# Two interleaved opening products, sums of squares by tokens, and small fp32 matmuls ahead of the first product and around the last sums

## The chip, the cores and the metric

The kernel runs on one core of one Trainium2 chip. The core has engines that run side by side, each with its own instruction queue, in order: TensorE (PE in the profile, with its weight loads as PEld), VectorE (DVE), ScalarE (ACT), GpSimd (POOL) and SyncE (SP), which here only starts transfers (DMAs). The metric is the device time in microseconds (us) of one execution, as a median of runs; lower is better.

## The reference

One inference step of an encoder trunk with two layers for 512 prompt tokens and 8 x 16 sample tokens, 640 tokens of width 1024 in all. Each layer is

```
x += 1/2 * SwiGLU_1(RMSNorm(x))
x += mixer(RMSNorm(x))          # short convolution, band attention, gates
x += 1/2 * SwiGLU_2(RMSNorm(x))
```

and a last RMSNorm follows. `RMSNorm(x) = x * rsqrt(mean(x*x) + 1e-6) * g`, and `SwiGLU(h) = (silu(h @ w_g) * (h @ w_u)) @ w_down` with an inner width of 2816. The mean is over the 1024 features of a token.

## The kernel before

x lies in SBUF by features: eight rows `x[0]` to `x[7]`, each 128 features (partitions) by T = 640 tokens. Products need fp32 accuracy and are made from a faster format (fp32r): an operand is split into a high part (a cast, on ScalarE) and a low part (the rest, a subtraction on VectorE), and one product of a 128 x 128 weight tile is three matmuls (high x high, low x high, high x low) for each half of the tokens (HT = 320). Since the norm's factor belongs to a token, i.e. a column, the products run on `x * g` and their results are scaled by the factor (rho) later.

Weights come as a stream of slabs of 128 x 1024 (512 KB), `wst`. `load` starts the transfer of a slab into one of a few buffers `raw` on SP's queue; `prep` casts it (`whi`) and notes the subtraction (`wlo`), which `flush` issues on VectorE; `slab` and `Tiles.take` hand the prepared slab out and prepare two ahead; `quiet` hands out without preparing. `wlo` and `whi` have three buffers each.

The first FFN of the first layer (`ffn("a0")`) starts with `opening` (L602): four inner tiles j, a gate and an up product each, so 2n = 8 products of 8 x 6 = 48 matmuls (L372). Each takes all eight rows of x. Their PSUM results are `acc` tiles of two banks, of which there are two (`layout("f", 1)`), so product i needs the buffer of product i - 2, which `out(i - 2)` has to have read: for the first pair a copy on ScalarE, for later ones a scaling by rho on VectorE (`scaled`, L487). The other four banks are `att` tiles. The rows of the opening run in the order in which they are written, on TensorE, VectorE and ScalarE (`order(ORDERED)`).

Before: x and the first slab come in alternating transfers (L415, L421). For each row, ScalarE and VectorE make its parts `hhi`, `hlo`, and for every second row two tiles of the first slab. Product 0 takes rows as they come; then product 1 with slab 1. Squares of the eight rows are made on ScalarE (L574) and added on VectorE (L578). Within product 2 the sums over features are made by ten small matmul instructions (`npsa`, L472), root and reciprocal follow, and the factors are put on a diagonal (L482); after the first row of product 3 a fp32 product with ones (`nbca`, L595) spreads them over the partitions, and ScalarE copies them to `rho` (L597). Meanwhile `final(m)` builds the operands `xhi`, `xlo` of the later inner tiles (seven combinations of row pairs: even row m in slots 5 and 6, odd row in 3 and 4, combinations of both in 0 to 2), spread over the products by the table `made`.

At the very end, `Final.all` (L1877) makes the last down product in two parts of the tokens (A, 384, and B, 256); it squares on ScalarE, sums over features by small matmuls with ones (`add`, L1936), takes root, reciprocal and diagonal (`root`, `turn`), spreads them (`spread`, L1952) and writes `yout` (`out`, L1957). The last rows of B end the kernel.

Of the kernel before, what the change touches and what calls it, by code (L numbers as in the profile page):

```python
# [10 lines left out]
F32 = mybir.dt.float32  # L11
# [5 lines left out]
P = 128  # L17
# [160 lines left out]


@with_exitstack  # L180
def trunk(ctx: ExitStack, tc: tile.TileContext, xin, wst, small, pbias, samplebias, kcache, vcache,
          yout, ko, vo, co):
    nc = tc.nc
    PE, DVE, ACT, POOL, SP = nc.tensor, nc.vector, nc.scalar, nc.gpsimd, nc.sync
# [123 lines left out]
    def flush():  # L308
        for lo, src, hi in pending:
            DVE.tensor_tensor(out=lo, in0=src, in1=hi.bitcast(F32), op=ALU.subtract)  # L310
        pending.clear()
# [94 lines left out]
    POOL.memset(epst, EPS)  # L406
    early = cp.tile([P, 1], F32, name="early")

    less = cp.tile([P, L * KT], F32, name="less")
    POOL.tensor_scalar(out=less, in0=sm[:, O_GM : O_GM + L * KT], scalar1=-1.0, scalar2=None, op0=ALU.mult)  # L410

# [2 lines left out]
    for k in range(KT):  # L414
        SP.dma_start(x[k], xin[:, k, :])  # L415

        if k == 0:
            raws.append(wp.tile([P, CH], F32, tag="raw", name="raw0", bufs=3))
        if k % 2 == 0:
            c = slice(k * P, (k + 2) * P)  # L420
            SP.dma_start(raws[0][:, c], wst[0][:, c])  # L421

    def norm(pool, name, goff, ssum):

# [64 lines left out]
    class Expand(Stats):  # L489
# [10 lines left out]
            self.sq = self.rest = None  # L500
            self.known = False

        def final(self, m, square=True):

            kp, odd = divmod(m, 2)
            n = f"{self.name}_{kp}"
            if not odd:

                self.E = self.fp.tile([P, 3, HT], F32, name=f"xe{n}", tag="even", bufs=1)
                hi = self.fp.tile([P, 7, HT], F32R, name=f"xhi{n}", tag=f"xhi{kp}")  # L510
                lo = self.fp.tile([P, 7, HT], F32R, name=f"xlo{n}", tag=f"xlo{kp}")
                self.ops.append((hi, lo))
# [8 lines left out]
            ACT.activation(B, halves(x[m]), AF.Copy, scale=g)  # L521
            if square and end:
                self.sq = tmp(f"sq{self.name}_{m}")
            elif square:
                self.square(m)
            if not odd:
                DVE.tensor_tensor(out=E[:, 1], in0=E[:, 0], in1=E[:, 2], op=ALU.subtract)
                self.flush()
                ACT.copy(hi[:, 5:7], E[:, 0:2])
                self.late.append((lo[:, 5:7], E[:, 0:2], hi[:, 5:7]))  # L530
            else:
                self.flush()
                ACT.copy(hi[:, 3:5], O[:, 3:5])
                for o, a, b in ((XN6, E[:, 1], O[:, 4]), (XT4, O[:, XN6], O[:, 3])):
                    DVE.scalar_tensor_tensor(out=O[:, o], in0=a, scalar=-1.0, in1=b,
                                             op0=ALU.mult, op1=ALU.subtract)
                DVE.tensor_tensor(out=O[:, XT7], in0=O[:, 4], in1=E[:, 2], op=ALU.subtract)
                self.late.append((lo[:, 3:5], O[:, 3:5], hi[:, 3:5]))
                self.flush()

                def rest():
                    ACT.copy(hi[:, 0:3], O[:, 0:3])
# [5 lines left out]
                if not end:  # L548
# [53 lines left out]
    def opening(fp, name, goff, n, put, tails):  # L602

        ACT.copy(early, epst)
        ex = Expand(fp, name, goff)
        h = []
        whi, wlo = (wp.tile([P, CH], F32R, tag=f"w{t}", name=f"w{t}0", bufs=3) for t in ("hi", "lo"))
        ready.append((whi, wlo))  # L610
        for k in range(KT):
            g = sm[:, goff + k : goff + k + 1]
            hi = hp.tile([P, T], F32R, tag="hhi", name=f"hhi{name}_{k}")
            lo = hp.tile([P, T], F32R, tag="hlo", name=f"hlo{name}_{k}")
            ACT.activation(hi, x[k], AF.Copy, scale=g)
            c = slice(k * P, (k + 2) * P)
            if k % 2 == 0:
                ACT.copy(whi[:, c], raws[0][:, c])
            DVE.scalar_tensor_tensor(out=lo, in0=x[k], scalar=g, in1=hi.bitcast(F32),
                                     op0=ALU.mult, op1=ALU.subtract)  # L620
            if k % 2 == 0:
                DVE.tensor_tensor(out=wlo[:, c], in0=raws[0][:, c], in1=whi[:, c].bitcast(F32),
                                  op=ALU.subtract)
            h.append((hi, lo))
        flush()

        made = {2: (0, 1), 3: (2, 3), 4: (4,), 5: (5, 6), 6: (7,)}
        us, gs, ps = [], [], []

        def out(i):  # L630

            j, up = divmod(i, 2)
            if not up:
                gs.append(tmp(f"g{name}_{j}"))
                if j:
                    scaled(gs[j], ps[i], ex.rho)
                    ACT.activation(gs[j], gs[j], AF.Silu)
# [11 lines left out]
        def begun():  # L649
            ex.total(att(f"nps{name}"))  # L650
            ex.root()
            ex.diagonal()

        at = {2: {4: begun}, 3: {1: lambda: ex.spread([att(f"nbc{name}_{a}")[:, :HT] for a in range(2)])}}
        for i in range(2 * n):
            ps.append(acc(f"po{name}_{i}"))
            product(ps[i], h, at.get(i, {}))
            if i > 1:
                out(i - 1)
            if i == 0:  # L660
                for k in range(KT):
                    ex.square(k)
                    ex.add()
                    if k == 1:
                        out(0)
                    if k == 4:
                        flush()
            if i == 1:
                continue
            if i == 3:  # L670
                g, u = gs[0], us[0]
                DVE.tensor_tensor(out=g, in0=g, in1=ex.rho, op=ALU.mult)
                ACT.activation(g, g, AF.Silu)
                DVE.tensor_tensor(out=u, in0=u, in1=ex.rho, op=ALU.mult)
            flush()
            for m in made.get(i, ()):
                ex.final(m, False)
            if i == 3:
                DVE.tensor_tensor(out=u, in0=u, in1=g, op=ALU.mult)
            if i == max(made):  # L680
                ex.rest()
        ahead()
        begin()
        out(2 * n - 1)

        def parts(j, u):
# [1181 lines left out]
    class Final:  # L1868
# [8 lines left out]
        def all(self, ops):  # L1877
# [9 lines left out]
            for m in range(KT):  # L1887
# [9 lines left out]
                    ACT.copy(rr, self.spread(0))  # L1897
                if m == 5:
                    self.ps = acc("npsf1")[:, :, 0]
                    self.add(self.ssum[1], True)  # L1900
                if m > 4:
                    self.add(self.sq)
# [158 lines left out]
def _layout(inputs):  # L2061
# [21 lines left out]
    return {"xin": xin, "wst": _stream(i), "small": small, "pbias": pbias, "samplebias": sbias, "kcache": kc, "vcache": vc}  # L2083


_OUTS = {
# [39 lines left out]
```

## Time and profile before

| | |
|---|---|
| median of three runs | 2496.47 us (2495.63 to 2496.84) |
| the profiled execution | 2496.66 us |
| its span, first to last instruction | 2494.7 us |
| mean granted TensorE clock | 0.998 |

The page of the profile gives the busy time of each engine, the chain of waits that ended last, and groups of instructions. Closer views are the timeline of one engine (start, duration, engine, line, operation, output <- inputs, shape, count, and in brackets the idle time before and what ended it), the chain within a stretch, and windows (busy time of each engine in order PE, PEld, DVE, ACT, POOL, then the granted clock, the share of the DMA engines and GB/s). Line numbers are those of the kernel before. Starts on one engine can lie closer together than the durations say, since instructions overlap in its pipeline.

### The profile page before, as it was taken

The numbers are of one execution on the slowest core, as the hardware profiler recorded it, in microseconds if no ns is written. First come the engines' busy times: TensorE is split into PE (matmuls) and PEld (weight loads), VectorE is DVE, ScalarE is ACT, GpSimd is POOL, SyncE is SP. The second block draws the span as 40 slices with busy tenths as digits, with TensorE's granted clock in tenths as the row PEclk, the third lists the DMA queues.
The fourth block names the chain that finished last, engine by engine and source line by source line (L and its number), as shares of the span: only waits on it lengthen the run. The fifth ranks groups of instructions, "written<-read, shape, count | busy, mean of one in ns | idle before, by whom it ended". The sixth has DMA issues, their size and how long they took to land.

```text
span 2494.7 us, 43515 instructions
## 1 busy us (share of the span) xinstructions
PE 2478.1 (99%) x17048; PEld 2419.0 (97%) x17048; DVE 2119.2 (85%) x3322; ACT 1450.0 (58%) x2343; POOL 370.7 (15%) x445
## 2 busy tenths in 40 slices
PE   9999999999999999999999999999999999999998
PEld 8999999888999999999999999998899999999998
DVE  7888888878888899888798889888788888989887
ACT  7455556674666555555565555556646665555554
POOL 0011211211111011111001111221111110111111
PEclk9999999999999999999999999999999999999999
DMA  4245665335345344655435555643344553455554
GB/s 146 82 107 124 138 135 130 106 115 167 99 119 145 101 116 118 138 135 135 117 90 126 129 134 123 138 119 115 125 153 104 126 141 95 119 133 122 129 135 110
DMA packets 133261, 308.10 MB, mean 124 GB/s; under 512 B 12768, under 2 KB 76128, under 8 KB 133056
## 3 DMA queue, kind: packets, MB, share of 16 engines
q1 hardware_dynamic: 68976, 219.18, 27.3%
q0 software_dynamic: 63360, 85.50, 20.6%
q8 instruction: 133, 2.18, 0.4%
q10 hardware_dynamic: 720, 0.65, 0.1%
q14 instruction: 72, 0.59, 0.1%
HBM read 221.13 MB, written 7.94 MB: 92 GB/s over the span
## 4 chain that ended last, share of the span: by engine, by line
PE 94%; DVE 3%; ACT 2%; DMA 1%; issue 0%; SPq 0%; DVEq 0%; ACTq 0%
PE pab L395 12%; PE paa L395 11%; PE pcb L395 6%; PE pca L395 6%; PE daa L962 5%; PE dab L962 5%; PE po L372 4%; PE qa L395 4%; PE pbb L395 3%; PE pba L395 3%; PE dca L962 3%; PE dcb L962 3%; PE pda L372 2%; PE pv L1622 2%; PE ma_cv L395 2%; PE qc L395 2%
## 5 line engine op out<-in xcount | busy, mean ns | idle before, releaser
L310 DVE TENSOR_TENSOR wlo<-raw,whi 128x512 fp32r<-128x512 f32 (+1 forms) x583 | 598.6, 1030 | 236.1 <-ACT whi L305 230.6
L305 ACT CAST whi<-raw 128x512 fp32r<-128x512 f32 (+1 forms) x583 | 519.9, 897 | 348.0 <-PE pbb L395 44.6
L305 ACT CAST whi<-s 128x1024 fp32r<-128x1024 f32 (+1 forms) x164 | 153.6, 937 | 248.1 <-issue 107.8
L395 PE MATMUL pab<-xhib,whi 128*128 128x320 f32 x704 | 218.3, 310 | 0.4 <-DVE gb L249 0.4
L395 PE MATMUL pab<-xhib,wlo 128*128 128x320 f32 x704 | 217.4, 309 | 0.0
L395 PE MATMUL pab<-xlob,whi 128*128 128x320 f32 x704 | 217.4, 309 | 0.0
L395 PE MATMUL paa<-xhia,whi 128*128 128x320 f32 x640 | 198.0, 309 | 0.2 <-DVE ga L249 0.2
L395 PE MATMUL paa<-xloa,whi 128*128 128x320 f32 x640 | 197.6, 309 | 0.0
L395 PE MATMUL paa<-xhia,wlo 128*128 128x320 f32 x640 | 197.6, 309 | 0.0
L310 DVE TENSOR_TENSOR wlo<-s,whi 128x1024 fp32r<-128x1024 f32 (+1 forms) x164 | 176.6, 1077 | 10.4 <-ACT whi L305 10.4
L395 PEld LDWEIGHTS pab<-xhib,whi 128*128 128x128 f32 x704 | 132.2, 188 | 1.1 <-DVE gb L249 0.9
L395 PEld LDWEIGHTS pab<-xlob,whi 128*128 128x128 f32 x704 | 132.2, 188 | 0.2
L395 PEld LDWEIGHTS pab<-xhib,wlo 128*128 128x128 f32 x704 | 132.2, 188 | 0.0
L395 PEld LDWEIGHTS paa<-xhia,whi 128*128 128x128 f32 x640 | 120.2, 188 | 0.5 <-DVE ga L249 0.5
L395 PEld LDWEIGHTS paa<-xloa,whi 128*128 128x128 f32 x640 | 120.2, 188 | 0.1
L395 PEld LDWEIGHTS paa<-xhia,wlo 128*128 128x128 f32 x640 | 120.2, 188 | 0.0
L249 DVE TENSOR_TENSOR raw<-raw,raw 128x512 f32<-128x512 f32 x164 | 112.2, 684 | 1.8 <-DMA raw<-in_wst 0.2
L249 DVE TENSOR_TENSOR raw<-s,raw 128x512 f32<-128x512 f32 x164 | 112.3, 685 | 0.0
L395 PE MATMUL pcb<-xhib,whi 128*128 128x320 f32 x352 | 108.7, 309 | 0.0
L395 PE MATMUL pcb<-xlob,whi 128*128 128x320 f32 x352 | 108.7, 309 | 0.0
L395 PE MATMUL pcb<-xhib,wlo 128*128 128x320 f32 x352 | 108.7, 309 | 0.0
L986 POOL DMA_DIRECT2D x<-c_b x52 | 62.6, 1203 | 309.5 <-ACT c_b L979 134.5
(816 smaller groups left out, 8170.8 us busy)
## 6 DMA issues: line engine op xcount, KB each, us to landing
raw<-in_wst SPq DMA_DIRECT2D x375, 512.0 KB, 3.7
x<-c_b POOLq DMA_DIRECT2D x52, 320.0 KB, 5.1
x<-c_a POOLq DMA_DIRECT2D x50, 320.0 KB, 5.0
kc<-in_kcache SPq DMA_DIRECT2D x32, 256.0 KB, 4.1
vc<-in_vcache SPq DMA_DIRECT2D x16, 512.0 KB, 4.5
ub<-cbb POOLq DMA_DIRECT2D x42, 160.0 KB, 5.9
ua<-cba POOLq DMA_DIRECT2D x38, 160.0 KB, 5.4
x<-u_a POOLq DMA_DIRECT2D x18, 320.0 KB, 5.1
```

What stands on the lines that cost most here:

```text
L249: DVE.tensor_tensor(out=out, in0=a, in1=b, op=ALU.add)
L305: ACT.copy(hi[:, d], src[:, c])
L310: DVE.tensor_tensor(out=lo, in0=src, in1=hi.bitcast(F32), op=ALU.subtract)
L372: PE.matmul(ps[a] if isinstance(ps, list) else ps[:, a, :HT], w, x[:, a * HT : (a + 1) * HT], start=first and j == 0, stop=last and j == 2)
L395: PE.matmul(ps, a, b, start=start and kp == 0 and j == 0, stop=stop and kp == NP - 1 and j == 2, skip_group_check=True)
L962: PE.matmul(ps[u], w, y, start=start and i == 0 and j == 0, stop=i == 1 and j == 2, skip_group_check=True)
L986: POOL.dma_start(rows(r, cols), z, accum_op=ALU.add)
L1622: PE.matmul(pv[t], xx[:, t * P : (t + 1) * P], w[:, kk * AW : (kk + 1) * AW], start=c == 0 and kk == 0 and j == 0, stop=c == KT // 2 - 1 a ...
```

## The change

A new input `xtok` holds x by tokens: five tiles of 128 tokens x 1024 features. In the opening:

- `stir` issues 24 fp32 matmuls of ones by ones (128 x 128 by 128 columns) on TensorE, into an `att` tile that nothing reads, ahead of the first product.
- Two slabs are loaded and split along with the rows of x, and products 0 and 1 are interleaved row by row (the last two rows together).
- The odd rows' parts are written to their place in `xhi`, `xlo` at once (`place`), and `final` with `whole=False` no longer makes them.
- The squares are summed over the features of a token by `square(c)`: instructions with an accumulated output, three token tiles on VectorE and two on ScalarE. `npsa` and the squares by rows are gone.
- `spread` and the scaling of the first pair stand after product 2, ahead of product 3, and `made` gives the finals one product earlier.

In `Final.all`, five such small matmuls stand ahead of the last addition to the sums, six behind it.

```diff
+    def stir(ps, n):
+        for _ in range(n):
+            PE.matmul(ps[:, :P], ones, ones, start=True, stop=True)
...
         if k == 0:
-            raws.append(wp.tile([P, CH], F32, tag="raw", name="raw0", bufs=3))
+            for n in range(2):
+                raws.append(wp.tile([P, CH], F32, tag="raw", name=f"raw{n}", bufs=3))
         if k % 2 == 0:
             c = slice(k * P, (k + 2) * P)
-            SP.dma_start(raws[0][:, c], wst[0][:, c])
+            for n in range(2):
+                SP.dma_start(raws[n][:, c], wst[n][:, c])
...
-        def final(self, m, square=True):
+        def final(self, m, whole=True, hold=False):
...
-                ACT.copy(hi[:, 3:5], O[:, 3:5])
+                if whole:
+                    ACT.copy(hi[:, 3:5], O[:, 3:5])
...
-                self.late.append((lo[:, 3:5], O[:, 3:5], hi[:, 3:5]))
+                if whole:
+                    self.late.append((lo[:, 3:5], O[:, 3:5], hi[:, 3:5]))
...
         ACT.copy(early, epst)
+        stir(att(f"stir{name}"), 24)
         ex = Expand(fp, name, goff)
+        ex.ps = fp.tile([P, NT], F32, name=f"sums{name}", bufs=1)
+        load(2)
...
+                SP.dma_start(z, xtok[c])
...
-                ACT.copy(whi[:, c], raws[0][:, c])
+            if not odd:
+                for (whi, _), raw in zip(ready, raws):
+                    (ACT.copy if k else DVE.tensor_copy)(whi[:, c], raw[:, c])
...
-        made = {2: (0, 1), 3: (2, 3), 4: (4,), 5: (5, 6), 6: (7,)}
+        made = {2: (1, 2), 3: (3, 4), 4: (5,), 5: (6, 7)}
...
-        at = {2: {4: begun}, 3: {1: lambda: ex.spread([att(f"nbc{name}_{a}")[:, :HT] for a in range(2)])}}
+        def square(c):
+            for z, total in toks[c]:
+                if c % 2 == 0:
+                    DVE.tensor_tensor_reduce(out=z, in0=z, in1=z, scale=1.0, scalar=0.0, op0=ALU.mult, op1=ALU.add,
+                                             accum_out=total)
+                else:
+                    ACT.activation(z, z, AF.Square, accum_out=total)
+
         for i in range(2 * n):
             ps.append(acc(f"po{name}_{i}"))
-            product(ps[i], h, at.get(i, {}))
-            if i > 1:
-                out(i - 1)
             if i == 0:
...
+                continue
             if i == 1:
-                continue
-            if i == 3:
+                ws = [[tiles.take() for _ in range(KT)]]
+                pair = quiet()
+                ws.append([tuple(z[:, k * P : (k + 1) * P] for z in pair) for k in range(KT)])
+                for ks in (*((k,) for k in range(KT - 2)), (KT - 2, KT - 1)):
+                    for p, w in zip(ps, ws):
+                        for k in ks:
+                            multiply(p, w[k], h[k], k == 0, k == KT - 1)
+                flush()
+                ex.final(0, False)
+                square(0)
+                out(0)
+                square(1)
+                square(2)
+                out(1)
+                square(3)
+                square(4)
+                add(ex.ps[:, 2:], ex.ps[:, 2:], rest)
+                ex.root()
+                ex.diagonal()
+                prep(len(ready))
+                flush()
+            else:
+                product(ps[i], h)
+                if i > 2:
+                    out(i - 1)
+            if i == 2:
+                ex.spread([att(f"nbc{name}_{a}")[:, :HT] for a in range(2)])
                 g, u = gs[0], us[0]
                 DVE.tensor_tensor(out=g, in0=g, in1=ex.rho, op=ALU.mult)
                 ACT.activation(g, g, AF.Silu)
...
             flush()
             for m in made.get(i, ()):
                 ex.final(m, False)
-            if i == 3:
+            if i == 2:
                 DVE.tensor_tensor(out=u, in0=u, in1=g, op=ALU.mult)
...
+                    self.idle = acc("stirf")[:, 0]
                     self.add(self.ssum[1], True)
...
+            stir(self.idle, 5)
             self.add(self.sq, False, True)
+            stir(self.idle, 6)
             self.root(1)
```

More of the change, by code (lines that the diff above doesn't have):

```diff
@@ L180, in trunk @@
 @with_exitstack
-def trunk(ctx: ExitStack, tc: tile.TileContext, xin, wst, small, pbias, samplebias, kcache, vcache,
+def trunk(ctx: ExitStack, tc: tile.TileContext, xin, xtok, wst, small, pbias, samplebias, kcache, vcache,
           yout, ko, vo, co):
@@ L501, in __init__, with place @@
             self.known = False
-        def final(self, m, square=True):
+        def place(self, kp):
+            self.ops.append(tuple(self.fp.tile([P, 7, HT], F32R, name=f"x{t}{self.name}_{kp}", tag=f"x{t}{kp}")
+                                  for t in ("hi", "lo")))
+        def final(self, m, whole=True, hold=False):
+            square = whole
             kp, odd = divmod(m, 2)
@@ L509, in final @@
                 self.E = self.fp.tile([P, 3, HT], F32, name=f"xe{n}", tag="even", bufs=1)
-                hi = self.fp.tile([P, 7, HT], F32R, name=f"xhi{n}", tag=f"xhi{kp}")
-                lo = self.fp.tile([P, 7, HT], F32R, name=f"xlo{n}", tag=f"xlo{kp}")
-                self.ops.append((hi, lo))
+                if whole:
+                    self.place(kp)
             else:
@@ L537, in final @@
                 DVE.tensor_tensor(out=O[:, XT7], in0=O[:, 4], in1=E[:, 2], op=ALU.subtract)
-                self.late.append((lo[:, 3:5], O[:, 3:5], hi[:, 3:5]))
+                if whole:
+                    self.late.append((lo[:, 3:5], O[:, 3:5], hi[:, 3:5]))
                 self.flush()
@@ L547, in final @@
                 self.rest = rest
-                if not end:
+                if not (end or hold):
                     rest()
@@ L606, in opening @@
         ACT.copy(early, epst)
+        stir(att(f"stir{name}"), 24)
         ex = Expand(fp, name, goff)
+        ex.ps = fp.tile([P, NT], F32, name=f"sums{name}", bufs=1)
+        load(2)
+        toks = []
+        rest = fp.tile([P, NT], F32, name=f"rest{name}", bufs=1)[:, : NT - 2]
+        for c in range(NT):
+            if c < 2:
+                z = fp.tile([P, D], F32, tag=("s65", "odd")[c], name=f"tok{name}_{c}", bufs=1)
+                toks.append([(z, ex.ps[:, c : c + 1])])
+                SP.dma_start(z, xtok[c])
+                continue
+            toks.append([])
+            for a, (tag, z) in enumerate((("hhi", ex.ps[:, c : c + 1]), ("hlo", rest[:, c - 2 : c - 1]))):
+                t = hp.tile([P, T], F32, tag=tag, name=f"tok{name}_{c}{a}")[:, : D // 2]
+                toks[c].append((t, z))
+                SP.dma_start(t, xtok[c][:, a * D // 2 : (a + 1) * D // 2])
@@ L608, in opening @@
         h = []
-        whi, wlo = (wp.tile([P, CH], F32R, tag=f"w{t}", name=f"w{t}0", bufs=3) for t in ("hi", "lo"))
-        ready.append((whi, wlo))
+        for n_ in range(2):
+            ready.append(tuple(wp.tile([P, CH], F32R, tag=f"w{t}", name=f"w{t}{n_}", bufs=3) for t in ("hi", "lo")))
         for k in range(KT):
             g = sm[:, goff + k : goff + k + 1]
-            hi = hp.tile([P, T], F32R, tag="hhi", name=f"hhi{name}_{k}")
-            lo = hp.tile([P, T], F32R, tag="hlo", name=f"hlo{name}_{k}")
+            kp, odd = divmod(k, 2)
+            if odd:
+                hi, lo = (z[:, 3:5].rearrange("p a b -> p (a b)") for z in ex.ops[kp])
+            else:
+                ex.place(kp)
+                hi = hp.tile([P, T], F32R, tag="hhi", name=f"hhi{name}_{k}")
+                lo = hp.tile([P, T], F32R, tag="hlo", name=f"hlo{name}_{k}")
@@ L615, in opening @@
             ACT.activation(hi, x[k], AF.Copy, scale=g)
             c = slice(k * P, (k + 2) * P)
-            if k % 2 == 0:
-                ACT.copy(whi[:, c], raws[0][:, c])
+            if not odd:
+                for (whi, _), raw in zip(ready, raws):
+                    (ACT.copy if k else DVE.tensor_copy)(whi[:, c], raw[:, c])
             DVE.scalar_tensor_tensor(out=lo, in0=x[k], scalar=g, in1=hi.bitcast(F32),
                                      op0=ALU.mult, op1=ALU.subtract)
-            if k % 2 == 0:
-                DVE.tensor_tensor(out=wlo[:, c], in0=raws[0][:, c], in1=whi[:, c].bitcast(F32),
-                                  op=ALU.subtract)
+            if not odd:
+                for (whi, wlo), raw in zip(ready, raws):
+                    DVE.tensor_tensor(out=wlo[:, c], in0=raw[:, c], in1=whi[:, c].bitcast(F32),
+                                      op=ALU.subtract)
@@ L647, in out @@
                 ACT.copy(halves(u), two(ps[i]))
[L649 to L652, printed above, removed]
-        at = {2: {4: begun}, 3: {1: lambda: ex.spread([att(f"nbc{name}_{a}")[:, :HT] for a in range(2)])}}
+        def square(c):
[5 more added lines that the diff above has]
+                    ACT.activation(z, z, AF.Square, accum_out=total)
         for i in range(2 * n):
             ps.append(acc(f"po{name}_{i}"))
-            product(ps[i], h, at.get(i, {}))
-            if i > 1:
-                out(i - 1)
             if i == 0:
[L661 to L667, printed above, removed]
-            if i == 1:
-                continue
-            if i == 3:
+                continue
+            if i == 1:
+                ws = [[tiles.take() for _ in range(KT)]]
[19 more added lines that the diff above has]
+                flush()
+            else:
+                product(ps[i], h)
[3 more added lines that the diff above has]
+                ex.spread([att(f"nbc{name}_{a}")[:, :HT] for a in range(2)])
                 g, u = gs[0], us[0]
@@ L2082, in _layout @@
     vc = i["cache_v"].reshape(L, NB, 2, P, AW).transpose(0, 1, 3, 2, 4)
-    return {"xin": xin, "wst": _stream(i), "small": small, "pbias": pbias, "samplebias": sbias, "kcache": kc, "vcache": vc}
+    return {"xin": xin, "xtok": tok.reshape(NT, P, D), "wst": _stream(i), "small": small, "pbias": pbias, "samplebias": sbias, "kcache": kc, "vcache": vc}
 _OUTS = {
```

1 line of the change is left out of this document (removed).

## The prediction

> **What bounds the kernel now.** First the page's head, then the chain of waits of the first 120 us, since the change touches only the opening and the last sums. Columns of the chain: start us, length us, what.
>
> ```profile
> span 2494.7 us, 43515 instructions
> PE 2478.1 (99%) x17048; PEld 2419.0 (97%) x17048; DVE 2119.2 (85%) x3322; ACT 1450.0 (58%) x2343; POOL 370.7 (15%) x445
> ...
> 13.92 1.06 ACT whi L305
> ...
> 15.01 1.24 DVE wlo L310
> ...
> 16.29 10.23 PE poa L372 x68
> 26.52 1.01 PE npsa L472 x10
> 27.53 4.51 PE poa L372 x30
> 32.04 1.08 PE nbca L595 x4
> 33.11 34.32 PE poa L372 x234
> 67.43 1.76 PE paa L395 x12
> ```
>
> TensorE is busy 99% of the span, so only time in which it starts late, runs slowly or stands still can be won. From 16.29 us on, the opening (eight products of 8 x 6 = 48 matmuls, 384 in all) runs on TensorE without a hole until 67.43: 68 + 30 + 234 = 332 matmuls, 1.01 us of small fp32 sums (npsa) and 1.08 us of the spread (nbca). One matmul takes 34.32 / 234 = 0.1467 us. So 332 x 0.1467 + 1.01 + 1.08 = 50.8 us; the seams add 0.3 us to reach 51.14. Ahead of 16.29 only 384 - 332 = 52 matmuls were done. TensorE's timeline shows why:
>
> ```profile
> 5.63 0.90 PE L372 MATMUL poa<-hhia,whi 128*128 128x320 f32 x2 [5.63 <-ACT whi L618]
> ...
> 7.49 0.73 PE L372 MATMUL poa<-hhia,whi 128*128 128x320 f32 x2
> 8.02 0.73 PE L372 MATMUL poa<-hloa,whi 128*128 128x320 f32 x2
> 8.55 0.63 PE L372 MATMUL poa<-hhia,wlo 128*128 128x320 f32 x2
> 9.02 0.46 PE L372 MATMUL poa<-hhia,whi 128*128 128x320 f32 x2
> 9.32 0.46 PE L372 MATMUL poa<-hloa,whi 128*128 128x320 f32 x2
> ```
>
> The first data are ready at 5.63. Pairs then start 0.53 us apart (7.49, 8.02, 8.55), and from 9.02 on 0.30: for its first 3.0 us TensorE runs at some 0.56 of its pace. After that the product waits for rows of x, and at 15.01 for the second slab's low part.
>
> **The change, part by part.** *The early small matmuls.* 24 fp32 products of 128 x 128 by 128 columns stand ahead of the first product on TensorE's queue. They need only the tile of ones:
>
> ```profile
> 0.88 0.21 POOL L404 MEMSET ones<- 128x128 f32 x1
> ```
>
> so they start at about 1.15. The trace has none of this shape. From below: npsa, ten instructions with one column in 1.01 us, 0.10 each, two to a product: 0.20. By columns: nbca, 1.08 us for two products of 320, gives 0.54 x 128 / 320 = 0.216. I take 0.216 at full pace and 0.216 x 0.53 / 0.30 = 0.38 at the early pace. With the slow phase as long as it was (3.0 us): 8 of them to 4.15, then 16 x 0.216 = 3.5, end 7.65. Slow twice as long: 16 to 7.15, then 1.7, end 8.9; slow throughout, 24 x 0.38 ends at 10.3; never slow, at 1.15 + 24 x 0.20 = 6.0. I take 8.0, as TensorE is idle until 1.15 in any case and the phase was seen once. The Trainium skill, "TensorE: Matmul & The Clock Gate" (Part 1), says that the clock opens after one busy window of about 3.4 us, that the windows run free, and that the start of a kernel therefore varies from run to run. By that rule the slow phase lies between 3.4 and 6.8 us, an end near 8.0 to 9.2; the trace's 3.0 us is just under it.
>
> *Two products at once.* With each row of x TensorE now has 12 matmuls, 12 x 0.1467 = 1.76 us. Loads by DMA ahead of the last row of x are 8 x 320 + 8 x 128 KB = 3584 KB, exactly what had landed (8 x 320 + 4 x 128 + 512) when the second slab's cast could start, at 13.92. Two rows cost ScalarE and VectorE:
>
> ```profile
> 4.46 0.83 ACT L615 ACTIVATE hhia<-x,sm 128x640 fp32r<-128x640 f32 x1 [1.79 <-DMA sm<-in_small]
> 5.19 0.39 ACT L618 CAST whi<-raw 128x256 fp32r<-128x256 f32 x1
> ...
> 6.12 0.42 DVE L622 TENSOR_TENSOR wlo<-raw,whi 128x256 fp32r<-128x256 f32 x1
> 6.78 0.89 DVE L619 SCALAR_TENSOR_TENSOR hloa<-x,sm,hhia 128x640 fp32r<-128x640 f32 x1 [0.24 <-ACT hhia L615]
> ```
>
> that is 2 x 0.83 + 2 x 0.39 = 2.4 and 2 x 0.89 + 2 x 0.42 = 2.6 us, under TensorE's 3.5. So from about 8.0 TensorE runs through, and both products end at 8.0 + 96 x 0.1467 = 22.1. (With no early matmuls the rows would bind instead, the third at about 10.5, which ends both products no earlier than 20.9, as if the start were 6.8; that is the lower bound.)
>
> *Squares by tokens.* 2.6 MB more by DMA, five squares shared by VectorE and ScalarE, no squares and additions by rows. TensorE loses npsa, 1.01 us. ScalarE's queue after product two (22.1) holds the second copy, 2.6 us of squares, the table load and root, then slab 3's cast; by the same rows I get slab 3's low part at about 28.8 and the reciprocals' tile at 27, against 29.1 (spread) and 30.3 (product four). Both are hidden, with some 1.5 us to spare; late, they would cost what exceeds that. The odd rows' parts go straight to their last place: four casts and four subtractions less, off the path.
>
> *The order after the third product is what I expect to cost.* There are two PSUM buffers for these products: the fifth may start only when VectorE has scaled the third out. Before, that scaling came first after the spread. These rows of VectorE and ScalarE show the old order and the prices:
>
> ```profile
> 36.17 0.82 DVE L487 TENSOR_TENSOR ga<-poa,rhoa 128x640 f32<-128x640 f32 x1 [1.93 <-ACT rhoa L597]
> 36.91 0.81 DVE L672 TENSOR_TENSOR ga<-ga,rhoa 128x640 f32<-128x640 f32 x1
> 37.65 0.82 DVE L674 TENSOR_TENSOR ua<-ua,rhoa 128x640 f32<-128x640 f32 x1
> 38.38 1.22 DVE L310 TENSOR_TENSOR wlo<-raw,whi 128x1024 fp32r<-128x1024 f32 x1
> 39.67 0.49 DVE L527 TENSOR_TENSOR xea<-xea 128x320 f32<-128x320 f32 x1
> 40.08 1.15 DVE L556 TENSOR_TENSOR xloa<-xoa,xhia 128x960 fp32r<-128x960 f32 x1
> 41.15 0.82 DVE L556 TENSOR_TENSOR xloa<-xea,xhia 128x640 fp32r<-128x640 f32 x1
> 42.13 0.49 DVE L535 SCALAR_TENSOR_TENSOR xoa<-xea,xoa 128x320 f32<-128x320 f32 x1 [0.17 <-ACT xoa L521]
> 42.66 0.49 DVE L535 SCALAR_TENSOR_TENSOR xoa<-xoa 128x320 f32<-128x320 f32 x1
> 43.07 0.48 DVE L537 TENSOR_TENSOR xoa<-xoa,xea 128x320 f32<-128x320 f32 x1
> ```
> ```profile
> 35.39 0.75 ACT L597 COPY rhoa<-nbca 128x320 f32<-128x320 f32 x2
> ...
> 38.82 0.82 ACT L521 ACTIVATE xea<-x,sm 128x640 f32<-128x640 f32 x1
> ...
> 43.58 0.99 ACT L542 CAST xhia<-xoa 128x960 fp32r<-128x960 f32 x1 [0.73 <-DVE xoa L537]
> 44.48 1.04 ACT L305 CAST whi<-raw 128x1024 fp32r<-128x1024 f32 x1
> ```
>
> Now the spread, both scalings of the first pair and the operands of rows 1 and 2 are written ahead of the fourth product's own step, so the scaling of the third product stands behind them all on VectorE. Starts lie about 0.08 closer than the durations. In us after the start Z of product four: rho at 0.75; two scalings, 1.48; a low weight part, 1.14; a low operand part, 0.74; three combinations, 1.34 (42.13 to 43.55 with the last's end): 5.5. ScalarE then casts the 960 wide part (0.90) and only after it makes row 2 (0.82), 7.3; VectorE subtracts 0.41, takes the 960 wide low part 1.07, multiplies the pair 0.74, and scales product three 0.82: 10.4. Product four ends at Z + 48 x 0.1467 = Z + 7.04. TensorE stands for 3.3 us. If VectorE never waited for ScalarE, its sum is 8.5 and the stall 1.45; if each ScalarE step came a microsecond late, 4.5. The sixth product then waits in the same manner: behind scaling three are eight more such steps, which by the same addition end 0.3 us after product five; two more seams, 0.1. I take 3.7 for all, between 1.5 and 4.5.
>
> *The last sums.* Columns as above, with the granted clock in the last window row:
>
> ```profile
> 2485.69 0.61 PE L1939 MATMUL npsf<-ones,sqf 128*128 128x1 f32 x4 [0.78 <-ACT sqf L1933]
> 2486.33 0.26 ACT L1944 ACTIVATE nrmsf<-npsf,epst 128x2 f32<-128x2 f32 x1 [0.69 <-PE npsf L1939]
> ...
> 2487.17 1.14 DVE L1958 SCALAR_TENSOR_TENSOR x<-x,sm,frr 128x384 f32<-128x384 f32 x2
> 2487.31 1.22 PE L1954 MATMUL nbcf<-fsum,ones 128*128 128x256 f32 x2 [1.02 <-DVE fsum L482]
> 2488.57 3.22 DVE L1958 SCALAR_TENSOR_TENSOR x<-x,sm,nbcf 128x256 f32<-128x256 f32 x8 [0.25 <-PE nbcf L1954]
> ```
> ```profile
> 2486.00:2488.00 2.00, 0.98 (x5) 0.70 (x4) 1.97 (x6) 0.26 (x1) 0.00 (x0) 0.75 0.86 308
> ```
>
> The granted clock falls to half in that window, and the last spread takes 1.22 us; at full pace 256 columns are about 0.7. Five small matmuls (1.1 us) fit between the last sums but one and 2485.69, six more (1.3) start near 2486.2 and end near 2487.5. The spread would end near 2488.2, but VectorE is at its two outputs until 2487.17 + 1.14 = 2488.31, so at most 0.26 us is won; I take 0.2. At half pace the six would end near 2488.6 and the spread near 2489.8: 1.3 us lost.
>
> **The sum.** The opening ends at 8.0 + 384 x 0.1467 (56.3) + 1.08 + 0.2 (seams) + 3.7 = 69.3, against 67.43: 1.9 later. Less 0.2 at the end: span 2494.7 + 1.7 = 2496.4. The profiled execution took 2496.66, 1.96 beyond its span, and lies 0.19 above the median of the runs shown; so 2496.47 + 1.7 = 2498.2.
>
> **Rivals.** *The third product's buffer is free in time* (VectorE gets to the scaling within 7 us): for it speaks that VectorE loses four subtractions, against it the sum of its own rows, 8.5. Then no stall: 2498.2 - 3.7 = 2494.5, faster than before, as it is for any stall under about 2.0. 17%. *The slow phase lasts through the early matmuls*, as it would if the windows fall badly or small fp32 products count little as activity: the product starts at 8.9 to 10.3, 2499.1 to 2500.5. The pace of 5.63 to 8.6 was reached under dense matmuls only. 15%. By the page's free windows (above) this is the run-to-run case. *The six late matmuls delay the last spread*: +1.5 on the forecast, 2499.7; 6%. *Odd rows now share a tile with parts written later, and products wait for that*: against it, TensorE read slices of whi at 5.63 while ScalarE wrote others later; it would cost several us in each of five products, over 2503. 4%.
>
> **How the numbers follow.** Forecast 58%. Its own range, stall 1.5 to 4.5 and start 7.65 to 8.9, is 2495.7 to 2499.9. With the first two rivals it becomes 2494.2 to 2500.8; outside are the shared tile and the corners where several mishaps add. What a measurement can tell here is 0.2%, 5 us: under 2491.5 would need an opening 5 us shorter, more than an opening with no stall and a start as good as 6.8 gives (67.43 - 6.8 - 56.3 - 1.3 = 3.0, and 0.26 at the end): 2%. Over 2501.5 needs stall and slow start together, or the shared tile: 7%. Within: 91%.
>
> **What would show it.** A first product that starts at 7.6 to 8.9 and runs through to about 22; no npsa on TensorE; slab 3 and the reciprocals in time; then, at about 37, a hole of some 3.3 us on TensorE ahead of the fifth product, ended by VectorE's scaling of the third (the line of the old L487), with a small one ahead of the sixth; the first matmul with paa at 69.3 instead of 67.43; a last spread of 0.7 us and a clock of 1.00 until 2488. No hole at 37, or paa before 67.4, proves the main step wrong.

## The result and the profile after

| | before | after |
|---|---|---|
| median, 18 runs each | 2496.51 us (2495.60 to 2497.30) | 2500.70 us (2499.54 to 2502.76) |
| the profiled execution | 2496.66 us | 2500.07 us |
| its span | 2494.7 us | 2498.3 us |

The ratio after / before is 1.0017, interval 1.0011 to 1.0024: the change costs 0.17%, about 4.2 us. The forecast was 2498.2 us, with a range from 2494.2 to 2500.8: the median lies 0.1 us inside it. The 18 runs of after lie in two groups, nine from 2499.54 to 2500.34 and nine from 2501.06 to 2502.76. The median falls into the gap; the profiled run is of the lower group.

The head of the page and the chain of waits of after's first 120 us (start us, length us, what):

```profile
span 2498.3 us, 43643 instructions
...
PE 2484.4 (99%) x17108; PEld 2426.9 (97%) x17108; DVE 2115.8 (85%) x3327; ACT 1442.9 (58%) x2338; POOL 370.1 (15%) x445
```
```profile
1.14 7.10 PE stira L411 x48
8.24 21.12 PE poa L372 x144
29.36 1.09 PE nbca L608 x4
...
40.66 29.93 PE poa L372 x192
70.59 1.76 PE paa L395 x12
```

The first three products run through, 144 matmuls at 21.12 / 144 = 0.1467 us each, npsa is gone, and the spread starts at 29.36. The opening ends at 70.59, where the first matmul into `paa` starts, instead of 67.43: 3.16 us later. Two losses, 3.2 and 1.8 us, explain it; without them it would end some 1.8 us ahead of before's. The fourth product would end at 29.36 + 1.09 + 7.04 = 37.5, yet the fifth starts at 40.66. And 192 matmuls at 0.1467 are 28.17 us, yet they took 29.93. The waits of TensorE (who waited for whom: us in total, times, longest) name the first; their second line, the wait in the gates, comes up again with the run same_3:

```profile
PE poa L372 <- DVE ga L493: 3.2, 1, 3.2
PE qa L395 <- ACT g L1382: 1.4, 2, 1.0
```

VectorE's timeline of after shows what stands ahead of the scaling of the third product (L493), in the order in which before's rows were shown:

```profile
30.93 0.82 DVE L725 TENSOR_TENSOR ga<-ga,rhoa 128x640 f32<-128x640 f32 x1 [2.75 <-ACT rhoa L610]
31.68 0.82 DVE L727 TENSOR_TENSOR ua<-ua,rhoa 128x640 f32<-128x640 f32 x1
...
37.48 0.49 DVE L538 TENSOR_TENSOR xea<-xea 128x320 f32<-128x320 f32 x1 [1.79 <-ACT xea L532]
37.89 1.15 DVE L569 TENSOR_TENSOR xloa<-xoa,xhia 128x960 fp32r<-128x960 f32 x1
38.96 0.82 DVE L732 TENSOR_TENSOR ua<-ua,ga 128x640 f32<-128x640 f32 x1
39.70 0.82 DVE L493 TENSOR_TENSOR ga<-poa,rhoa 128x640 f32<-128x640 f32 x1
```

Before, the scaling came first after the spread; now it is the last of this list, and VectorE itself stands 1.79 us for ScalarE in the middle of it. The windows of after give the second loss (length; busy time and count of PE, PEld, DVE, ACT, POOL; granted clock; DMA share; GB/s):

```profile
41.00:42.00 1.00, 1.00 (x9) 1.00 (x8) 1.00 (x2) 1.00 (x2) 0.00 (x0) 0.90 0.00 0
42.00:43.00 1.00, 1.00 (x5) 1.00 (x5) 0.96 (x3) 0.01 (x1) 0.00 (x0) 0.50 0.48 66
43.00:44.00 1.00, 1.00 (x5) 1.00 (x5) 0.71 (x2) 0.25 (x1) 0.00 (x0) 0.50 0.79 291
44.00:45.00 1.00, 1.00 (x6) 1.00 (x5) 0.00 (x0) 1.00 (x2) 0.00 (x0) 0.50 0.42 168
45.00:46.00 1.00, 1.00 (x8) 1.00 (x7) 0.50 (x2) 0.47 (x1) 0.00 (x0) 0.89 0.00 0
```

TensorE is busy in every microsecond, but the count, in which those cut by an edge are included, falls from 9 to 5 or 6: some 1.2 us after the hole the granted clock goes to 0.50 and stays there until about 45.2. A busy share of 1.00 hides this; the count and the clock column show it. The last rows of after's timeline at the end of the kernel:

```profile
2489.83 0.51 PE L1995 MATMUL npsf<-ones,sqf 128*128 128x1 f32 x4
2490.20 1.58 PE L411 MATMUL stirf<-ones 128*128 128x128 f32 x12
...
2491.21 1.14 DVE L2014 SCALAR_TENSOR_TENSOR x<-x,sm,frr 128x384 f32<-128x384 f32 x2
2491.62 0.60 PE L2010 MATMUL nbcf<-fsum,ones 128*128 128x256 f32 x2
2492.27 3.22 DVE L2014 SCALAR_TENSOR_TENSOR x<-x,sm,nbcf 128x256 f32<-128x256 f32 x8
```

The last spread takes 0.60 instead of 1.22 us, and the last outputs start right behind VectorE's two earlier ones. So the span's 3.6 us are 3.16 of the opening, 0.7 net that came in between, and some 0.2 won back at the end. In between TensorE has one kind of wait that before's list does not have, for the gates: 1.0 us in the first layer and 0.4 in the second. The 0.7 is what is left of them; part of the first is won back within 25 us, where before has a wait that after does not.

### The profile page after: what moved, and what is told of

The parts are those of the page before. It is cut to its first block, busy times and chain, and to the rows that moved or that the text cites. A ratio compares the mean times of both kernels' runs of the same rounds, so it can differ in the third digit from the quotient of the medians.

```text
span 2498.3 us, 43643 instructions
## 1 busy us (share of the span) xinstructions
PE 2484.4 (99%) x17108; PEld 2426.9 (97%) x17108; DVE 2115.8 (85%) x3327; ACT 1442.9 (58%) x2338; POOL 370.1 (15%) x445
## 4 chain that ended last, share of the span: by engine, by line
PE 95%; DVE 3%; ACT 2%; issue 0%; DMA 0%; DVEq 0%; POOL 0%; ACTq 0%; POOLq 0%
PE pab L395 12%; PE paa L395 11%; PE pcb L395 6%; PE pca L395 6%; PE daa L1015 5%; PE dab L1015 5%; PE po L372 4%; PE qa L395 4%; PE pbb L395 3%; PE pba L395 3%; PE dcb L1015 3%; PE dca L1015 3%; PE pda L372 2%; PE pv L1675 2%; PE ma_cv L395 2%; PE poa L372 2%
## 5 line engine op out<-in xcount | busy, mean ns | idle before, releaser
L310 DVE TENSOR_TENSOR wlo<-raw,whi 128x1024 fp32r<-128x1024 f32 (+1 forms) x582 | 597.5, 1030 | 236.6 <-ACT whi L305 230.5
L305 ACT CAST whi<-raw 128x1024 fp32r<-128x1024 f32 (+1 forms) x582 | 518.8, 896 | 349.2 <-PE pbb L395 43.1
L310 DVE TENSOR_TENSOR wlo<-s,whi 128x1024 fp32r<-128x1024 f32 (+1 forms) x164 | 176.7, 1077 | 10.3 <-ACT whi L305 10.3
```

The lines of the kernel that those rows point to most:

```text
L305: ACT.copy(hi[:, d], src[:, c])
```

## The experiments

Theory: the hole ahead of the fifth product is the order of the rows on VectorE and ScalarE; the halved clock behind it is the hole's own consequence; the early and late small matmuls cost next to nothing. Rivals: the clock falls for another reason, at that time of the kernel; or the loss comes from the small matmuls or from the interleaving. Edits are against after unless it is said otherwise. All times are medians, with the ratio to before, which was run again beside each (medians 2496.69 to 2496.98), and its interval. `same_again`, `same_2` and `same_3` are after, unchanged, run again.

**scaling_later.** The scalings of the first pair move behind the scaling of the third product; `made` stays.

```diff
+            if i == 3:
                 g, u = gs[0], us[0]
                 DVE.tensor_tensor(out=g, in0=g, in1=ex.rho, op=ALU.mult)
...
-            if i == 2:
+            if i == 3:
                 DVE.tensor_tensor(out=u, in0=u, in1=g, op=ALU.mult)
```

> The scalings of the first pair (and its product) move behind the scaling of the third product; the operands' order (made) stays. Theory (VectorE's written order decides when the PSUM buffer is free): the third product's scaling still stands behind the operands of rows 1 and 2, so a hole of about 1.6 us stays ahead of the fifth product, and the moved steps now delay the fourth product's scaling: a new hole of about 2.5 us ahead of the sixth. Sum of holes 4.1 against 3.2, the opening ends within 1 us of the changed kernel's, unless shorter holes no longer bring the slow pace (then 1.7 us earlier). Rival (the early scalings alone are the cause): no hole, the opening ends near 66 us.

2501.21 us (10 runs), ratio 1.0018 [1.0009, 1.0027]. Its waits of TensorE, and a part of its windows:

```profile
PE poa L372 <- DVE ua L493: 2.2, 1, 2.2
...
PE poa L372 <- DVE ga L493: 1.3, 1, 1.3
```
```profile
49.00:50.00 1.00, 1.00 (x7) 1.00 (x7) 1.00 (x2) 0.00 (x0) 0.00 (x0) 0.84 0.00 0
50.00:51.00 1.00, 1.00 (x6) 1.00 (x5) 1.00 (x2) 0.00 (x0) 0.00 (x0) 0.50 0.00 0
...
53.00:54.00 1.00, 1.00 (x8) 1.00 (x8) 0.45 (x1) 1.00 (x2) 0.00 (x0) 0.95 0.30 119
```

The hole ahead of the fifth product shrinks from 3.2 to 1.3 us, and a new one of 2.2 appears ahead of the sixth, behind what was moved: as expected in kind, each 0.3 shorter. The queue's length is paid one product later. Counted from the first product's start, the opening takes 0.6 us more than after's. The halved clock moves with the larger hole, to behind 48.8, and does not come at 42. That rules out a cause that belongs to a fixed time of the kernel.

**order.** As scaling_later, and the operands of the later tiles come one step later, too.

```diff
-        made = {2: (1, 2), 3: (3, 4), 4: (5,), 5: (6, 7)}
+        made = {2: (1,), 3: (2, 3), 4: (4,), 5: (5, 6), 6: (7,)}
```

> As the one before, and the operands again one product later: made = {2: (1,), 3: (2, 3), 4: (4,), 5: (5, 6), 6: (7,)}. Theory: no hole between the products and no slow pace behind it; the opening ends at 65.8 us instead of 70.6, the median is 2496 or a little under it, 4.8 us under the changed kernel, and the runs lie within 1.5 us. Rival (the slow pace has another cause, such as the early small matmuls or the transfers of the token tiles): the hole goes, 3.2 us, but TensorE still runs at half its pace for some 3 us, 2497.5.

2495.97 us (11 runs), ratio 0.9995 [0.9986, 1.0004]. Its chain:

```profile
1.14 7.69 PE stira L411 x48
8.82 21.12 PE poa L372 x144
29.94 1.08 PE nbca L608 x4
31.02 35.20 PE poa L372 x240
66.22 1.76 PE paa L395 x12
```

All 240 matmuls of the last five products run at 35.20 / 240 = 0.1467, without hole or halved clock. The opening ends 4.37 us before after's although its first product starts 0.58 later. Both of the opening's losses are thus the place of those rows, and the interleaving, which stays, is not to blame. The operands' place alone was not run, so how much of the gain needs both moves is open.

**hole_filled.** After, with 13 small matmuls in the hole, so that TensorE is busy while it waits.

```diff
                 product(ps[i], h)
+                if i == 3:
+                    stir(att(f"hole{name}"), 13)
                 if i > 2:
```

> The changed kernel with 13 small fp32 matmuls of ones behind the fourth product: 13 x 0.23 = 3.0 us of work in the hole, the order of all else untouched. Theory (the hole has a second price, since the clock is halved for a window after it): the fifth product still starts at 40.6, but runs at full pace; the opening ends at 68.8 us instead of 70.6, the median falls by 1.7 us or more, and the runs no longer spread over 3 us. Rival (the slow pace is not the hole's): 70.6 us and 2500.7 as before, or later by what the fill adds.

2499.46 us (11 runs), ratio 1.0011 [1.0002, 1.002]. Its chain from the fifth product on, and one of its windows:

```profile
40.78 7.27 PE poa L372 x48
...
48.07 21.54 PE poa L372 x144
69.61 1.76 PE paa L395 x12
```
```profile
43.00:44.00 1.00, 1.00 (x9) 1.00 (x8) 0.84 (x2) 0.13 (x1) 0.00 (x0) 1.00 0.76 287
```

The fifth product still waits as long (it starts at 40.78), but the clock stays at 1.00: so it is TensorE's idleness in the hole that halves it. (Luck of the kind that spared same_3, below, is not the reason: by the windows worked out in the last section, an unfilled hole would have left 2.1 us of idle time in one window here, about as much as in same_2, where the clock fell.) The median is 1.85 us under that of same_again, as expected, but the opening's share of it is smaller than expected. From the end of the early matmuls to paa it is 61.25 us against 62.35 in after, 1.1 less and not 1.8. At full pace the same 192 matmuls take 28.81 us, 0.64 over their sum: the seams that the slower pace had covered come out, among them a wait of 0.3 of the sixth product. In the profiles the rest comes behind the opening, where this run's list has 0.2 us of waits for the gates, after's 1.4.

**same_again.** After unchanged.

> The changed kernel once more, for a second profile. Its 18 runs fall in two groups, 2499.5 to 2500.3 and 2501.1 to 2502.8. If the clock's window is what differs, a profile of the upper group shows a second stretch at half pace, or a longer one, and the same hole; a profile of the lower group shows the same 3.4 us as the first.

2501.31 us (10 runs), ratio 1.0019 [1.001, 1.0028]. Hole 3.2, 192 matmuls in 29.93, paa at 70.94: as in after, 0.35 later, as its first product is (8.58).

**order_stir17 and order_nostir.** The order of `order`, with 17 early small matmuls or none.

```diff
-        stir(att(f"stir{name}"), 24)
+        stir(att(f"stir{name}"), 17)
```

> The order of before the hole, with 17 early small matmuls instead of 24. Theory (24 are too many: the first rows are ready at 6.8 to 7.4 us, the small matmuls end at 8.2 to 8.8): 17 end at 6.6 to 7.1, the first product starts there, rows then bind as if it were 6.8; the opening ends at 64.3 to 64.9 instead of 66.2, the median is 2494.3, 1.7 under the kernel with 24 and 2.2 under the kernel before. Rival (the rows bind anyway): no change, 66.2 and 2496.0.

> The same order with no early small matmuls. Theory: the product starts with the first rows at 6, its first 3 us run at half pace (1.5 us lost), the rest at full pace: first pair done at about 21.6, the opening ends near 65.0, 2494.8: better than 24, a little worse than 17. Rival (what the small matmuls do for the clock is worth more than they cost): later than 66.2 and over 2496.0.

With 17: 2493.19 us (11 runs), ratio 0.9986 [0.9977, 0.9995], paa at 64.75, against 66.22 with 24 in order. With none: 2495.42 (11 runs), 0.9994 [0.9985, 1.0003]. The chain of order_nostir:

```profile
6.74 22.82 PE poa L372 x142
...
65.83 1.76 PE paa L395 x12
```

Without them the product starts at 5.82, earliest of the kernels with the new opening, but goes through the early pace itself, which lasted until 10.6 here and not for the expected 3 us, and its opening ends 1.08 behind that of 17. So the early matmuls do pay, if there are not more of them than the early phase needs; after's 24 run on at full pace while the first rows of x are waiting. The theory's "next to nothing" was wrong for these: the seven beyond 17 cost some 1.5 us.

**before_stir and before_tail.** One part of the change alone, put into before: the 24 early matmuls; the five and six late ones.

```diff
         ACT.copy(early, epst)
+        stir(att(f"stir{name}"), 24)
```
```diff
+            stir(self.idle, 5)
             self.add(self.sq, False, True)
+            stir(self.idle, 6)
```

> The kernel before with the 24 early small matmuls alone. Theory: product 0 waits for rows of x and product 1 for the second slab's low part at 16.25 us in any case, so a start at 8.2 to 8.8 at full pace changes nothing: first matmul after 16.29 and first paa at 67.43, each within 0.3 us, the median within 0.6 of the kernel before. Rival (the slow first 3 us are on the path): 1.2 us earlier.

> The kernel before with the eleven small matmuls around the last sums alone. Theory: the clock stays at 1.00, the last spread takes 0.6 instead of 1.2 us, and the eight last outputs start 0.2 to 0.26 us earlier behind the last but one output, counted from the last product; median 0.2 lower, too little for the timing to tell. Rival (the six behind the sum delay the spread): outputs later than before.

2496.49 us (10 runs), ratio 1.0 [0.999, 1.0009], and 2496.62 (11 runs), 0.9999 [0.999, 1.0008]: neither can be told from before by its time. In the traces the first ends its opening at 67.03, 0.4 earlier than before's 67.43 and slightly more than the expected 0.3. The second has the short last spread:

```profile
2487.53 0.60 PE L1961 MATMUL nbcf<-fsum,ones 128*128 128x256 f32 x2
2488.18 3.21 DVE L1965 SCALAR_TENSOR_TENSOR x<-x,sm,nbcf 128x256 f32<-128x256 f32 x8
```

The last group of the down product but one starts at 2482.46 in before's chain and at 2482.23 in this one. From there to the last outputs it is 2488.57 - 2482.46 = 6.11 us in before and 2488.18 - 2482.23 = 5.95 here: 0.16 less. In after the same group starts at 2486.32 and the outputs at 2492.27, 5.95 as well. By the traces the late small matmuls cost nothing and win about what was forecast.

**order_stir14.** The order of `order`, 14 early matmuls.

> The order without the hole and 14 early small matmuls. With 17 they ended at 7.36 us (half pace until about 5.6), the rows allow a start at about 6.8. Theory (what the early small matmuls cost is the delay beyond the rows): 14 end near 6.6, the opening ends 0.3 to 0.7 us earlier than with 17 (64.75), 2492.7. Rival (the clock now opens only after the product has started, or the rows bind): the same as with 17 within 0.3 us, or later.

2493.26 us (11 runs), ratio 0.9986 [0.9977, 0.9995]. Its chain:

```profile
6.87 21.12 PE poa L372 x144
...
64.26 1.76 PE paa L395 x12
```

The opening ends half a microsecond before that of 17; the medians cannot be told apart. Both beat before, by 3.5 and 3.8 us, and after.

**same_2 and same_3.** After unchanged, one profile each, to see what makes the two groups of runs.

> The changed kernel, one more profile. If free windows of about 3.4 us set the clock, then the end of the early half pace and the half pace behind the hole move together from run to run, by whole windows from one to the other (in the first profile 4.5, 41.9 and 45.2 us: 37.4 is 11 windows of 3.4). A run of the upper group (over 2501) then shows a later end of the early half pace, up to 3.4 us later, which costs up to 1.7 us; the hole itself stays 3.2 us.

> The changed kernel, another profile with the same expectation: the hole ahead of the fifth product is 3.2 us in every run; what differs between runs is where the clock's windows fall, seen in the end of the early half pace and in the stretch behind the hole.

same_2 took 2500.39 us, at the upper edge of after's lower group, with a hole of 3.2 and 192 matmuls in 29.93. same_3 took 2502.24, of the upper group. Its chain, and its list of waits:

```profile
1.14 7.79 PE stira L411 x48
8.93 21.11 PE poa L372 x144
...
41.35 7.28 PE poa L372 x48
...
48.63 21.55 PE poa L372 x144
70.19 1.76 PE paa L395 x12
```
```profile
PE poa L372 <- DVE ga L493: 3.2, 1, 3.2
PE qa L395 <- ACT g L1382: 2.4, 2, 2.1
```

The expectation for the upper group was a miss: the early phase does last longer, but this opening ends 0.4 us before after's, since the same hole is not followed by a halved clock here. What makes this run longer lies in the first layer's gates, in code that the change leaves alone. Windows of same_3 there:

```profile
755.00:760.00 5.00, 5.00 (x36) 5.00 (x35) 3.06 (x6) 1.57 (x3) 1.04 (x1) 1.00 0.56 120
760.00:765.00 5.00, 2.92 (x16) 2.66 (x15) 3.51 (x6) 3.50 (x6) 0.91 (x1) 0.85 0.21 37
765.00:770.00 5.00, 5.00 (x30) 5.00 (x29) 3.14 (x5) 2.16 (x5) 2.62 (x3) 0.81 0.88 220
```

TensorE stands for 2.1 us, and again the clock falls behind it: 30 matmuls in 5 us where 36 are usual. In after, the longest stand there is 1.0 us and the clock stays at 1.00. The chain of same_3 leads from the matmul back to VectorE, which waits for a slab of weights:

```profile
751.34 5.47 DMA raw<-in_wst
...
756.90 0.70 DVE raw L249
```

In after that link is 4.42 us long; in before, VectorE's first operation on the slab follows the one ahead of it without a wait. By the chain, the slab's landing decides, and the other profiles bear it out. Wherever the link stands in the chain of that stretch, TensorE's longest wait for the gates grows with it:

| | the slab's link (us) | longest wait (us) |
|---|---|---|
| order_stir14 | 3.80 | 0.4 |
| order_stir17 | 3.82 | 0.4 |
| same_again | 4.23 | 0.8 |
| after | 4.42 | 1.0 |
| order | 4.47 | 1.1 |
| scaling_later | 4.68 | 1.3 |
| same_2 | 4.70 | 1.3 |
| same_3 | 5.47 | 2.1 |

Why the slab takes longer in one run than in another is not settled: its time follows neither the opening's end nor its edits, and differs between runs of the same kernel.

That is one run of the upper group. For the others only times and mean clocks are recorded. The mean clock is 0.998 in eight of the nine runs of after's upper group and 0.999 or 1.000 in all nine of the lower one. An estimate: one more stretch of 3.41 us at half pace takes 0.0007 off the mean. A further stretch at half pace is therefore likely in them; where it lies is not shown.

The profiled executions side by side (us):

| | opening ends | span | span less opening |
|---|---|---|---|
| before | 67.43 | 2494.7 | 2427.3 |
| before_stir | 67.03 | 2494.2 | 2427.2 |
| before_tail | 67.30 | 2494.4 | 2427.1 |
| order | 66.22 | 2493.4 | 2427.2 |
| order_nostir | 65.83 | 2492.6 | 2426.8 |
| order_stir17 | 64.75 | 2492.2 | 2427.5 |
| order_stir14 | 64.26 | 2491.3 | 2427.0 |
| hole_filled | 69.61 | 2496.8 | 2427.2 |
| after | 70.59 | 2498.3 | 2427.7 |
| same_again | 70.94 | 2498.6 | 2427.7 |
| same_2 | 70.67 | 2498.6 | 2427.9 |
| scaling_later | 71.70 | 2499.7 | 2428.0 |
| same_3 | 70.19 | 2500.5 | 2430.3 |

What the opening wins or loses reaches the end: the last column stays within 0.7 us of before's 2427.3, and same_3 alone adds 3 us.

## Why the prediction was right, and where its sum was off

- **Start of the first product.** Forecast 8.0 (7.65 to 8.9); measured 8.24 in after, and up to 8.93 (same_3) over the profiles with 24 of them. The mechanism (a phase at some half the pace, then full pace) was right, and the second rival's 8.9 was touched once. By the traces' record of the granted clock (a list of stretches with start, length and clock, which begins where the early phase ends), the phase ended at 4.26 us in after and at 5.72 in same_3; half of this difference is the 0.7 us by which their products start apart. By the Trainium skill, "TensorE: Matmul & The Clock Gate" (Part 1), where that first phase ends depends on where a free-running window falls; the spread of 0.7 us over the runs agrees.
- **Two products through, npsa gone, squares by tokens hidden.** All as worked out: 0.1467 us per matmul from 8.24 to 29.36, with no wait. The rival of a tile shared with later parts is gone with it.
- **The hole ahead of the fifth product.** Forecast 3.3 us, ended by the scaling of the third product; measured 3.2 in all four profiles of after's code. scaling_later and order show that it is the order of the rows that makes it. The first rival, no stall, failed.
- **What the step left out.** "I take 3.7 for all" counted only the time in which TensorE stands, and the sum priced all 384 matmuls at 0.1467. Behind the hole, 192 matmuls took 29.93 instead of 28.17: the clock was halved, 1.76 us. The 0.4 forecast for the sixth product and the seams did not appear on top, as the slower pace covered them; where the clock stayed at 1.00 (hole_filled, same_3) they were 0.65. The net error of the term is therefore 1.1; with a start 0.24 later than 8.0 the opening ended at 70.59, forecast 69.3. The prediction used the clock gate for the kernel's start and its last sums, and not for the hole that it forecast itself.
- **The last sums.** Forecast 0.2 won, spread at 0.7 us; the spread took 0.60, and outputs started 0.2 us nearer to the work ahead of them. The rival that they delay the last spread failed.
- **The middle.** Nothing was forecast between opening and end. Net 0.7 us in the profiled run, and 3 us in same_3, came in there, in the main from the gates' wait for a slab. With the clock behind the hole, this is why the median, 2500.70, lies 2.5 us over the forecast.
- **What was luck.** The direction and the hole were forecast by their mechanism; that the range holds the median was luck. The forecast's own range ended at 2499.9, 0.8 us under the median. The wider one reached 2500.8 in the main for a late start of the first product, up to 10.3, which did not come: it left room, by 0.1 us, for a halved clock and a wait that the sum did not have.

## What to carry to other kernels

When an edit makes the busiest engine stand, price the pace behind the hole as well as the hole: look for the granted clock after an idle stretch of comparable length anywhere in the same trace (here the last sums of the kernel before had shown it). When rows are moved ahead on an in-order queue, sum everything that then stands ahead of the one row that frees a buffer; moving part of it behind that row only pays if the next buffer's row doesn't inherit it, as it did in scaling_later. A warm-up is worth what the slow phase would cost the real work, less the delay of its start, and each instruction beyond that is paid: with none, 14, 17 and 24 the opening ended at 65.83, 64.26, 64.75 and 66.22 us.

## What the hardware showed that was not expected

- **A hole of 2.2 us halves the clock for 3.4 us.** In scaling_later TensorE stood from 46.6 to 48.8, and the clock was at 0.50 from 49.7 to 53.1. In same_3's opening a hole of 3.2 us, longer, was followed by no halved clock. An estimate from the traces: the record of the granted clock begins at 4.26 us in after, 4.98 in same_again, 5.31 in scaling_later and 5.72 in same_3. The first fall of the clock lies 37.5 us behind this in the first two, 44.4 in the third and 757.8 (in the gates) in the fourth: 11, 13 and 222 times 3.413. With this grid the last whole window ahead of the halved clock held 2.3 us of idle time in after, 1.9 in same_again, 2.2 in scaling_later and 2.1 in same_3's gates; in same_3's opening the hole was split into about 1.7 and 1.5. So it looks as if the idle share of one window decides, at about half of it. The end of the kernel before shows that this is not the whole rule: there the clock fell at 2487.0, 726 such windows after its record began (8.93), behind a window with only 1.5 us of idle time, beside 1.2 us of matmuls with a single column; whether those count as activity is not shown. The Trainium skill, "TensorE: Matmul & The Clock Gate" (Part 1), gives a free-running window of 3413 ns, which agrees, and an idle window of about 3.4 us as the condition, which is more than the 1.9 to 2.3 us of idle time that were enough here.
- **The early phase is not in the granted-clock column.** Windows of order_nostir:

```profile
6.00:8.00 2.00, 1.98 (x7) 1.58 (x8) 2.00 (x4) 1.43 (x2) 0.00 (x0) 1.00 1.04 348
8.00:10.00 2.00, 2.00 (x9) 2.00 (x9) 1.71 (x4) 1.57 (x4) 0.00 (x0) 1.00 1.01 316
10.00:12.00 2.00, 2.00 (x14) 2.00 (x13) 1.88 (x3) 1.52 (x4) 0.00 (x0) 1.00 1.01 355
```

The column says 1.00 throughout, while 7 and 9 matmuls are done in 2 us and then 14. The record of this trace begins only at 10.6, and there the starts go from 0.27 to 0.15 us apart. At the start of a kernel the pace is read from the counts.
- **Small fp32 matmuls count as activity.** 48 instructions of 128 x 128 by 128 columns brought TensorE to its full pace in after (three to 0.2 us at first, four to five from 4.2 us on), and 26 of them kept the clock at 1.00 in hole_filled.
